# Six branch-gate weights as a seven-product stage ahead of attention, the norm of the mixing in place, fill units and modulation columns dealt out anew

## The chip, the cores and the metric

One Trainium2 chip, one of its cores. The time is device microseconds (us) for one launch, which computes one layer of the model below. Several runs of a kernel give a median; besides them one execution was recorded by the profiler, and all durations and counts of instructions are from that one.

Engine names as in the profile: PE is TensorE (matmuls), PEld its loading of weights, DVE is VectorE, ACT is ScalarE, POOL is GpSimd, SP is SyncE, which issues most of the transfers. An engine takes its instructions in the order in which the program has put them, so an instruction that waits holds back all that stands behind it on its engine.

## The reference

One inference step of one trunk layer, for 640 tokens (128 of a prompt and 512 latents), a model width of 1024, and a feed-forward width of 2816. All inputs are float32.

```python
x = x + 0.5 * m[2] * swiglu(rmsnorm(x, g[0]) * (1 + m[1]) + m[0], ffn1)   # FFN 1
hh = rmsnorm(x, g[1]) * (1 + m[4]) + m[3]          # the norm of the mixing
mq, mk, mv, mo, mg, dq, dk, dv, gm, gd = split_cols(hh @ w_in)
dq, dk = rmsnorm(dq, g_qn), rmsnorm(dk, g_kn)      # then rope_2d for the latents
att = diff_attention(dq, keys, vals, lam)          # 8 heads, 2 softmaxes each, 5 query blocks of 128
hm  = mlstm, forward and backward, on mq, mk, mv with gates mg; 4 heads, chunks of 128
hm  = rmsnorm(hm) * sigmoid(mo)
y   = sigmoid(gm) * (hm @ w_br_m) + sigmoid(gd) * (att @ w_br_d)
x   = x + m[5] * (y @ w_out)
x   = x + 0.5 * m[8] * swiglu(rmsnorm(x, g[2]) * (1 + m[7]) + m[6], ffn2)  # FFN 2
```

m are nine modulation vectors, silu(c) @ w_ada + b_ada, one set for the prompt and one for the latents. Of the products of hh, each of mq, mk, mv, mo, gm, gd is 1024 wide. gm and gd, the branch gates, are only needed in y, at the end of the mixing.

## The kernel before

**Numbers.** Each float32 matrix is split into a high and a low part of the type fp32r, H = copy(x) on ACT and L = x - H on DVE, and a product is three matmuls, H·H, H·L and L·H, into one accumulation (`mm3`, `into`). hh is held as hH and hL, features on the 128 partitions, 8 k-tiles by 640 tokens, in two halves of 320 tokens (`HALF`).

**Weights** come in granules of 1024 x 256 (raw, 1 MB), which are loaded by a DMA, split by one ACT copy and one DVE subtraction, and used as a feature granule or as a token granule. A feature granule has four units of 24 matmuls of 320 columns (`feat_unit`, names ps_p); a token granule has five units of 24 matmuls of 256 columns (`tok_unit`, ps_t). A unit ends with an evacuation of its result from its bank to memory.

**Seven-product form** (class `HalfStep`, `products` L441). In the up stage of FFN 1 and in FFN 2 a granule of 256 features by 640 tokens by 1024 is computed as 2 x 2 blocks in Winograd's form with seven products instead of eight: 84 matmuls of 320 columns (ps_f) instead of 96. For that, sums and differences are needed: four of the operand, once (`operand_sums`, tiles S, 128x640), and four of each weight granule (`Granule.parts`: wB, wC and three differences in place in raw; `Granule.sums`: the last split, ww or wL). They are made on DVE and ACT while the granule before it is being multiplied. Results leave through `done(mt, hf, p, u)`, a copy or a sum with a saved part u.

**Stages**, in the order of TensorE's queue:
1. The opening (0 to 76 us): modulation and the norm of FFN 1.
2. FFN 1 up (76 to 340), then down (340 to 465). While it runs, DVE makes modulation columns too (`Columns`, L720): each of 56 tiles is loaded as 128x1024 and takes a pair of DVE instructions of that size. 14 are placed in the up stage, 18 in the down granules, 14 in attention and 10 in the memory phase (`columns.place(n)`, `columns.tile()`).
3. The norm of the mixing. `to_mixing` (called for each of 8 features tiles d and both halves) gathers squares; x is stored in x_dram with two transfers, one for each half. `norm2` calls `norm_apply` for each d and half: nt = x · scale · rstd on DVE, hH = nt + shift on ACT, hL = nt + shift - hH on DVE. The second half of that runs among the first token units (`norm2_second`).
4. The first query and key projections, as groups of token units (`tok_group`, q0 and k0), their norms and rotations (`qk_norm_rope`, L1290; "rope" below) and tables for them, then the sixteen small products of the mLSTM's gates (`gate_products`, mg, not the branch gates).
5. Attention (518 to 1075): eight heads of five query blocks. For each block TensorE makes scores, the transposes of the block before (`turn`, ps_wT) and its values (`values`, ps_o); between, ACT makes exponentials and DVE the minima (`mn`), the mixing of both softmaxes (`mix`, p) and the turns' copies. Scores stand in banks of their own, which are free again when the exponentials have read them.
6. The memory phase (1075 to 1250): the mLSTM's cells, with fill units between.
7. Branch outputs, w_out (1250 to 1413), FFN 2 (1413 to 1836).

**Fill units** (class `Fill`). The other projections (v, the later q and k, mq, mk, mv, mo, gm, gd) stand in one queue of granules, and `fill.units(n)` puts their next n units on TensorE, so that it has work while DVE and ACT make the softmax. How many stand where is a hand-written table `UNITS`: for each head a pair for every query block (units before and after `mix` and `values`), and a last entry for the end of the head. `fill.ahead()` splits the next granules' weights, which puts a DVE subtraction of 128x2048 (wL) into DVE's queue.

```python
for qi in range(5):
    n = UNITS[hd][qi]
    ... H.scores(qi); H.turn(qi - 1); H.soft(qi)
    aside(hd, qi, 0)            # a modulation tile, in some blocks
    fill.units(n[0])
    ... H.mix(qi); H.values(qi - 1)
    ... heads[hd + 1].pack()    # at qi == 3: queries and keys of the next head
    fill.units(n[1])
    fill.ahead()
```

Where text stands as `with tc.issue_after(i)` or `with written()`, it fixes that the instructions come behind others in their engine's queue; the rest is ordered by a scheduler as the program is built.

Of the kernel before, what the change touches and what calls it, by code (L numbers as in the profile page):

```python
# [31 lines left out]
def tile_trunk(ctx: ExitStack, tc: tile.TileContext, a: dict):  # L32
# [187 lines left out]
    def norm_apply(x, n, m_shift, hf, d, rs, hH, hL, tmp):  # L220
        c0 = hf * HALF
        shift = m_of(m_shift)
        for s0, s1, j in SEGS[hf]:
            t = tmp.tile([128, HALF], F32, tag="nt", name="nt", bufs=2)
            tv = t[:, : s1 - s0]
            stt(tv, x[d][:, s0:s1], scale[:, n, d, j : j + 1], rs[:, s0 - c0 : s1 - c0], ALU.mult, ALU.mult)
            sh = shift[:, d, j : j + 1]
            act(hH[:, d, s0:s1], tv, AF.Identity, bias=sh)
            ins = stt(hL[:, d, s0:s1], tv, sh, hH[:, d, s0:s1].bitcast(F32), ALU.add, ALU.subtract)
        return ins.ins  # L230

# [94 lines left out]
    class HalfStep:  # L326
        def __init__(self, n, fp, tmp, psum, w1, w3, w2, n_plain):

            self.n_plain = n_plain
            self.fp, self.tmp, self.psum, self.w1, self.w3, self.w2 = fp, tmp, psum, w1, w3, w2  # L330
            hm = [hp.tile([128, 2, 2, 4, HALF], F32R, tag=t, name="hm") for t in ("hH", "hL")]

            self.part = {(0, 0): hm[0][:, 0], (1, 0): hm[0][:, 1], (1, 1): hm[1][:, 0], (0, 1): hm[1][:, 1]}
            self.g_dram = dp.tile([4 if n_plain == FB else 7, 128, 2, FB, HALF], F32, name=f"g_dram{n}")
            self.up = [
                Granule(4, lambda raw, src=src: dma(raw, src)) for b in range(1, FB) for src in (w1[b], w3[b])
            ]

        def hh(self, k, hf):
            p = self.part[k // 4, hf]  # L340
            return p[:, 0, k % 4], p[:, 1, k % 4]


        def plain(self, p, w, f, hf, k):

            col = k * 256 + f * 128
            mm3(p, w[0][:, col : col + 128], w[1][:, col : col + 128], *self.hh(k, hf), k == 0, k == KT - 1)

        def begin_gated(self, b):
            self.Q, n = (PLAIN_Q, 4) if b < self.n_plain else (Q, 8)  # L350
            self.SO = self.fp.tile([128, 8, HALF], F32, tag="SO", name="SO")[:, :n]

        def silu_tile(self, f, hf):
            return self.tmp.tile([128, HALF], F32, tag=("nsq", "nt")[f], name="s", bufs=2)

        def gate_plain(self, f, hf, p):
            s = self.silu_tile(f, hf)
            self.at_act = act(s, p[0], AF.Silu)
            tt(vec, self.SO[:, self.Q[f, hf]], p[1], s, ALU.mult)

        def operand_sums(self, pair):

            SS = {i: self.fp.tile([128, 2, 4, HALF], F32R, tag=f"s{i}", name="S") for i in (S1, S2, S3)}
            SS[S4] = self.part[0, 1]
# [42 lines left out]
        def store_g(self, SO, b):  # L407

            n = 4
            if b >= self.n_plain:  # L410
                self.gated_sums(SO)
                n = 7
            for tag, c0, c1 in (("gA", 0, 4), ("gB", 4, 7)):
                if c0 < n:
                    g = self.fp.tile([128, 2, c1 - c0, HALF], F32R, tag=tag, name="g")
                    act(g[:, 0], SO[:, c0:c1], AF.Copy)
                    tt(vec, g[:, 1], SO[:, c0:c1], g[:, 0].bitcast(F32), ALU.subtract)
                    for i in range(2):
                        nc.sync.dma_start(out=self.g_dram[c0:c1, :, i, b, :].rearrange("s p n -> p s n"), in_=g[:, i].bitcast(F32))

        def gated_sums(self, SO):
            tt(vec, SO[:, S1], SO[:, A21], SO[:, A22], ALU.add)
            tt(vec, SO[:, S3], SO[:, A11], SO[:, A21], ALU.subtract)
            tt(vec, SO[:, S2], SO[:, S1], SO[:, A11], ALU.subtract)
            tt(vec, SO[:, S4], SO[:, A12], SO[:, S2], ALU.subtract)


# [13 lines left out]
        def products(self, work, between, then=(), ahead=None, prepared=False):  # L441
# [14 lines left out]
            for i, (gr, A, done, used) in enumerate(work):  # L456
# [14 lines left out]
                X, Y, Z = acc_tile(psum), acc_tile(psum), acc_tile(psum)  # L471
                into(X, A11, True)
# [38 lines left out]
        def add(self, p, u):  # L511
            t = self.tmp.tile([128, HALF], F32, tag="nrt", name="t")
            tt(vec, t, p, u, ALU.add)
            return t

# [221 lines left out]
    with ExitStack() as ph:  # L737
# [254 lines left out]
        def modulation(i, at):  # L992
# [10 lines left out]
            elif i < 28:  # L1003
                if (i, at) == (20, 0):
# [168 lines left out]
    ap = att.enter_context(tc.tile_pool(name="att", bufs=1))  # L1173
# [6 lines left out]
    def gate_products():  # L1180
        raw = load(rawp, [128, KT, 128], a["w_g"], tag="raw", name="wg_raw")
        wgH = ap.tile([128, KT, 128], F32R, tag="kH", name="wgH")
        wgL = ap.tile([128, KT, 128], F32R, tag="kL", name="wgL")
# [106 lines left out]
    def qk_norm_rope(raw, tab):  # L1290
        A, B, g = tab
        sq = ap.tile([128, 5, 256], F32, tag="pk", name="sq", bufs=2)
        act(sq, raw, AF.Square)
        ss = ap.tile([128, 20], F32, tag="ss", name="ss", bufs=2)
        vec.tensor_reduce(out=ss, in_=sq.rearrange("p t (g d) -> p (t g) d", d=64), axis=AX.X, op=ALU.add)
        rs = rstd_of(ap, ss, 1.0 / 64, [128, 20], "qk")
        r3 = raw.rearrange("p t (g d) -> p (t g) d", d=64)
        tt(vec, r3, r3, rs[:, :, None].to_broadcast([128, 20, 64]), ALU.mult)
        sw = ap.tile([128, 4, 256], F32, tag="pk", name="sw", bufs=2)
# [15 lines left out]
    def project_q(pr):  # L1315
        def make():
            q_tok[pr] = t = ap.tile([128, 5, 256], F32, tag="qtok", name="q_tok")

            def evac(p, i):
                act(t[:, i, :], p, AF.Copy)  # L1320
                if i == 4:
                    qk_norm_rope(t, tabs[0])

            return evac

        return a["w_dq"][pr], make

    def project_k(pr):
        def make():
            k_tok[pr] = t = ap.tile([128, 5, 256], F32, tag="ktok", name="k_tok")  # L1330

            def evac(p, i):
                act(t[:, i, :], p, AF.Copy)
                if i == 4:
                    qk_norm_rope(t, tabs[1])
                    nc.sync.dma_start(out=a["new_k"][:, pr * 256 : (pr + 1) * 256], in_=t[:, 4, :])

# [18 lines left out]
    class Head:  # L1356
# [5 lines left out]
        def pack(self):  # L1362
            self.pack_queries(ap, 2)
            self.pack_keys()

        def pack_queries(self, pool, bufs):
# [3 lines left out]
            self.qpk = pool.tile([128, 5, 4, 64], F32R, tag="pk", name="qpk", bufs=bufs)  # L1370
# [70 lines left out]
        def mix(self, qi):  # L1441
# [3 lines left out]
            stt(r, sm[:, 0:1], nlam, rc[:, 1:2], ALU.mult, ALU.mult)  # L1445
# [34 lines left out]
        def finish(self):  # L1480
            aT = ap.tile([128, T], F32, tag="asq", name="aT")
            for i0, n in ((0, 4), (4, 1)):
# [3 lines left out]
                act(aT[:, i0 * 128 : (i0 + n) * 128], p.rearrange("p a b -> p (a b)")[:, : n * 128], AF.Copy, scale=gs)  # L1486
            nc.sync.dma_start(out=aT_dram[:, self.hd, :], in_=aT)


    (src_q, e_q), (src_k, e_k) = project_q(0), project_k(0)  # L1490
    e_q, e_k = e_q(), e_k()
    w_q = split_w(src_q)
    with tc.issue_after(stats[1].at_act.ins), tc.issue_after(stats[1].at_vec.ins):
        w_k = split_w(src_k)

    def norm2_second(k):
        if k == 2:
            box["normed"] = norm2(psum, 1)

    tok_group(psum, [(w_q, 0, e_q), (w_q, 1, e_q)], norm2_second)  # L1500
    tok_group(psum, [(w_k, 0, e_k), (w_k, 1, e_k)], lambda k: None)
    with tc.issue_after(box["normed"]):
        ps_g, gate_step = gate_products()

    tab0 = ap.tile([128, 4, 4, 64], F32, tag="pk", name="tab0", bufs=2)
    cosT, sinT, lamv = tab0[:, 0], tab0[:, 1], tab0[:, 2]
    g_q, g_k = (load(ap, [128, 64], a[n].partition_broadcast(128), name=n) for n in ("g_qn", "g_kn"))
    ts(g_q, g_q, -0.125, ALU.mult)
    with tc.issue_after(box["normed"]):
        nc.sync.dma_start(out=cosT, in_=a["cos"])  # L1510
        nc.sync.dma_start(out=sinT, in_=a["sin"])
        nc.sync.dma_start(out=lamv, in_=a["lam"].partition_broadcast(128))
        gs = load(ap, [128, 1], a["g_sub"], name="gs")
        ts(gs, gs, 1.0 - LAM_INIT, ALU.mult)

        ldot = ap.tile([128, 2], F32, name="ldot")
        for i in range(2):
            vec.tensor_tensor_reduce(
                out=tab0[:, 3, i, :], in0=lamv[:, 2 * i, :], in1=lamv[:, 2 * i + 1, :], op0=ALU.mult, op1=ALU.add,
                scale=1.0, scalar=0.0, accum_out=ldot[:, i : i + 1],  # L1520
            )
        lexp = ap.tile([128, 2], F32, name="lexp")
        act(lexp, ldot, AF.Exp)
# [695 lines left out]
```

## Time and profile before

| | |
|---|---|
| median of three runs | 1840.3 us (1836.87 to 1843.62) |
| the profiled execution's own time | 1838.32 us |
| its span in the profile | 1836.5 us |
| TensorE clock granted, mean | 0.998 |
| busy: PE, DVE, ACT | 98%, 70%, 46% of the span |
| instructions: PE, DVE, ACT | 12,678, 2,110, 1,451 |
| HBM over the span | 162 GB/s |

The page of the profile lists busy time by engine, the span in 40 slices, the chain of work that ended last, and the groups of instructions by program line, with their form: output<-inputs, partitions x elements, type, count. Other views of the same trace are used below: busy time by stretches of the span; groups by line with each form apart; waits by the tile that was waited for and the engine that delivered it (time in us, count, longest); the instructions of a stretch one by one, start and duration first, with a wait in square brackets; and the chain that ended last in its order of time, each piece with its start, its length and how many instructions it holds. A helper records most operations, so L75 is every matmul, L78 every transpose, L51 every ACT operation, L54 every DVE tensor_tensor, L57 every scalar_tensor_tensor: the tile's name tells them apart. TensorE's matmuls overlap in the records, so their mean durations don't add up to its time.

### The profile page before, as it was taken

Reading aid. Unit: us, or ns where it says so; the run is one execution under the profiler, and the core shown is the slowest. Engines: PE = TensorE matmul, PEld = TensorE weight load, DVE = VectorE, ACT = ScalarE, POOL = GpSimd, SP = SyncE. Lnnn points to the kernel's source line nnn. Section 1 sums busy time; section 2 is a strip of 40 time slices with the busy share of each in tenths; the row PEclk is TensorE's granted clock in tenths of the full one; section 3 lists DMA queues with packets and bytes.
Section 4 is the critical chain, followed back from the end, with each engine's and each line's share of the span. In section 5 each row is a group of like instructions: output and inputs, shape, how many; then the busy total and the mean of one; then the engine's idle time right before and its main releaser. Section 6 shows DMA issues by size and latency. Waiting matters only on the chain.

```text
span 1836.5 us, 30726 instructions
## 1 busy us (share of the span) xinstructions
PE 1802.6 (98%) x12678; PEld 1764.6 (96%) x12678; DVE 1282.8 (70%) x2110; ACT 844.2 (46%) x1451; POOL 30.9 (2%) x55
## 2 busy tenths in 40 slices
PE   7999999999999999999999999999999999999999
PEld 5999999999999999999999999999999999999999
DVE  5899886577785767765745457874456878887575
ACT  4644444112554444544544455565235555554232
POOL 0000001010000000000000000000000000000000
PEclk9999999999999999999999999999999999999999
DMA  7364457964324233232222255564532345447872
GB/s 290 120 222 164 172 176 273 379 212 152 110 103 146 96 117 105 104 103 82 71 75 88 76 179 161 189 226 178 182 134 86 133 153 188 170 166 260 313 289 84
DMA packets 127902, 299.83 MB, mean 163 GB/s; under 512 B 9553, under 2 KB 90705, under 8 KB 114961
## 3 DMA queue, kind: packets, MB, share of 16 engines
q1 hardware_dynamic: 118498, 257.49, 40.7%
q0 software_dynamic: 9264, 40.37, 6.0%
q8 instruction: 100, 1.64, 0.4%
q14 instruction: 40, 0.33, 0.1%
HBM read 234.20 MB, written 63.63 MB: 162 GB/s over the span
## 4 chain that ended last, share of the span: by engine, by line
PE 83%; DVE 7%; DMA 6%; ACT 2%; issue 1%; SPq 0%; DVEq 0%; ACTq 0%
PE ps_f L75 40%; PE ps_p L75 22%; PE ps_t L75 12%; PE sc L75 2%; PE ps_o L75 2%; DMA ada<-csil_dram 1%; DVE ww L54 1%; PE ps_n L75 1%; DMA raw_a<-in_w_ada_k 1%; PE ps_wT L78 1%; PE ps_qkT L78 1%; DMA raw<-in_w3a 1%; DVE raw_a L720 1%; DMA P<-nm_dram 1%; PE ps_u L75 1%
## 5 line engine op out<-in xcount | busy, mean ns | idle before, releaser
L75 PE MATMUL ps_f<-S,ww 128*128 128x320 f32 x1956 | 314.3, 310 | 6.8 <-DVE ww L54 3.7
L75 PEld LDWEIGHTS ps_f<-S,ww 128*128 128x128 f32 x1956 | 293.1, 188 | 9.7 <-DVE ww L54 6.9
L75 PE MATMUL ps_p<-hH,wH 128*128 128x320 f32 x864 | 273.3, 316 | 2.0 <-ACT num L51 0.7
L75 PE MATMUL ps_p<-hH,wL 128*128 128x320 f32 x864 | 267.0, 309 | 0.0
L75 PE MATMUL ps_p<-hL,wH 128*128 128x320 f32 x864 | 266.9, 309 | 0.0
L75 PE MATMUL ps_f<-hm,ww 128*128 128x320 f32 x1236 | 194.3, 309 | 2.4 <-DVE ww L54 2.1
L75 PEld LDWEIGHTS ps_f<-hm,ww 128*128 128x128 f32 x1236 | 184.4, 188 | 3.0 <-DVE ww L54 2.4
L75 PE MATMUL ps_t<-wH,hH 128*128 128x256 f32 x640 | 185.3, 290 | 1.0 <-DVE x L57 1.0
L51 ACT ACTIVATE ww<-raw 128x2048 fp32r<-128x2048 f32 (+1 forms) x61 | 114.1, 1870 | 150.0 <-PE ps_f L75 86.3
L75 PE MATMUL ps_t<-wH,hL 128*128 128x256 f32 x640 | 181.2, 283 | 0.0
L75 PE MATMUL ps_t<-wL,hH 128*128 128x256 f32 x640 | 180.9, 283 | 0.0
L75 PEld LDWEIGHTS ps_p<-hH,wH 128*128 128x128 f32 x864 | 162.4, 188 | 3.4 <-ACT num L51 1.1
L75 PEld LDWEIGHTS ps_p<-hL,wH 128*128 128x128 f32 x864 | 162.4, 188 | 0.5
L75 PEld LDWEIGHTS ps_p<-hH,wL 128*128 128x128 f32 x864 | 162.2, 188 | 0.0
L54 DVE TENSOR_TENSOR ww<-raw,ww 128x2048 fp32r<-128x2048 f32 (+1 forms) x61 | 136.3, 2235 | 35.0 <-ACT ww L51 35.0
L75 PE MATMUL ps_f<-hm,wB 128*128 128x320 f32 x984 | 157.6, 309 | 0.0
L75 PEld LDWEIGHTS ps_f<-hm,wB 128*128 128x128 f32 x984 | 147.7, 188 | 0.0
L54 DVE TENSOR_TENSOR wL<-raw,wH 128x2048 fp32r<-128x2048 f32 x49 | 112.2, 2290 | 39.0 <-ACT wH L51 38.3
L75 PEld LDWEIGHTS ps_t<-wH,hH 128*128 128x128 f32 x640 | 122.3, 191 | 2.0 <-issue 1.2
L54 DVE TENSOR_TENSOR raw<-raw 128x1024 f32<-128x1024 f32 x141 | 121.7, 863 | 1.8
L75 PEld LDWEIGHTS ps_t<-wH,hL 128*128 128x128 f32 x640 | 122.4, 191 | 0.5 <-DVE hL L57 0.5
L75 PEld LDWEIGHTS ps_t<-wL,hH 128*128 128x128 f32 x640 | 122.5, 191 | 0.2
(294 smaller groups left out, 3185.8 us busy)
## 6 DMA issues: line engine op xcount, KB each, us to landing
g_dram<-g SPq DMA_DIRECT2D x44, 640.0 KB, 5.9
raw_a<-in_w_ada_c SPq DMA_DIRECT2D x24, 512.0 KB, 4.1
raw<-in_w1b SPq DMA_DIRECT2D x11, 1024.0 KB, 4.9
raw<-in_w3b SPq DMA_DIRECT2D x11, 1024.0 KB, 4.9
raw<-in_w1a SPq DMA_DIRECT2D x10, 1024.0 KB, 4.8
raw<-in_w3a SPq DMA_DIRECT2D x10, 1024.0 KB, 6.4
ada<-in_w_ada_c POOLq DMA_DIRECT2D x18, 512.0 KB, 4.9
hm<-g_dram POOLq DMA_DIRECT2D x7, 1280.0 KB, 10.5
```

Of the source, the lines that this page charges most:

```text
L51: return placed(nc.scalar.activation(*args, **kw))
L54: return placed(eng.tensor_tensor(out=out, in0=in0, in1=in1, op=op))
L75: tc.keep_in_program_order(nc.tensor.matmul(*args, **kw))
L78: tc.keep_in_program_order(nc.tensor.transpose(*args, **kw))
L720: placed(vec.tensor_tensor_reduce(out=junk, in0=raw, in1=self.csil[:, v, :], op0=ALU.mult, op1=ALU.add, scale=1.0, scalar=0.0, accum_out=m ...
```

## The change

1. **Six granules of the branch gates** (gd and gm, column groups 0, 1 and 2 of four) leave the fill queue and the memory phase's units and become a stage of their own, in seven-product form, after `gate_products` and before attention. `HalfStep`'s methods for it go into a base class `Winograd`; a new class `Gates` uses them. In each of its first two granules one matmul more is issued, into a bank that is overwritten (`narrow=2`). Operand sums are made of the normed x, which is held in place for that.
2. **The norm of the mixing** (`norm2`): no `norm_apply`. x is multiplied by rstd in place in pairs of d (4 DVE instructions of 128x640 for each half), ACT makes hH from it with scale and bias, x itself is scaled and shifted in place (first half on ACT, second on DVE), and hL = x - hH in pairs. x_dram is stored in eight parts, one for each pair of d and half, as soon as the pair's residuals are there.
3. **Tables and the ropes of q0 and k0** wait in a list and are issued in the new stage, behind the weight splits of its granules.
4. **Modulation columns**: 21 tiles instead of 18 in the down granules of FFN 1, 11 instead of 14 in attention, 10 in the memory phase as before.
5. **Fill queue** in a new order. v0, mo0, mv0, mq0, q1 and so on come in attention; mk3, mo2, mo3, gm3 and gd3 are left for the memory phase (5 granules, 20 units, as many as before, where mk3 is now evacuated by ACT). Nine units stand ahead of head 0's first block instead of seven, and `UNITS` is written anew with fewer units for each head.
6. **Packing**: both parts of head 0's pack are issued at once; the next head's pack comes at block 4 before `mix` for odd heads instead of at block 3.

```diff
-    class HalfStep:
+    class Winograd:
...
+                if i < narrow:
+                    mm(Y, gr.w[A11][0][0], A(A11)[:, 0, 0], start=True, stop=True)
                 into(X, A11, True)
...
+    class HalfStep(Winograd):
...
-                    columns.place(18, csil, load_columns)
+                    columns.place(21, csil, load_columns)
                 columns.tile(hs.at_vec)
-                if at and i in (22, 25):
+                if at and i < 25:
                     columns.tile(hs.at_vec)
...
-            if stats[hf].n == KT:
-                dma(x_dram[:, :, half(hf)], box["x"][1][:, :, half(hf)])
+            if d % 2:
+                dma(x_dram[:, d - 1 : d + 1, half(hf)], box["x"][1][:, d - 1 : d + 1, half(hf)])
...
         def norm2(psum, hf):
             rs = stats[hf].rstd(psum)
-            for d in range(KT):
-                ins = norm_apply(x, 1, 3, hf, d, rs, *hh2, ntmp)
-            return ins
+            xa, (hH, hL), shift = box["x"][1], hh2, m_of(3)
+            for g in range(4):
+                xs = xa[:, 2 * g : 2 * g + 2, half(hf)]
+                tt(vec, xs, xs, rs[:, None, :].to_broadcast([128, 2, HALF]), ALU.mult)
+                for d in (2 * g, 2 * g + 1):
+                    for s0, s1, j in SEGS[hf]:
+                        xd, sc, sh = xa[:, d, s0:s1], scale[:, 1, d, j : j + 1], shift[:, d, j : j + 1]
+                        act(hH[:, d, s0:s1], xd, AF.Identity, scale=sc, bias=sh)
+                        if hf == 0:
+                            act(xd, xd, AF.Identity, scale=sc, bias=sh)
+                        else:
+                            ts(xd, xd, sc, ALU.mult, sh, ALU.add)
+                ins = tt(vec, hL[:, 2 * g : 2 * g + 2, half(hf)], xs, hH[:, 2 * g : 2 * g + 2, half(hf)].bitcast(F32), ALU.subtract)
...
-        columns.place(14, csil, load_columns, 1)
+        columns.place(11, csil, load_columns, 1)
...
+    class Gates(Winograd):
+        def __init__(self, fp, tmp, psum):
+            self.fp, self.tmp, self.psum = fp, tmp, psum
+            self.part = {(kh, hf): Of(kh, hf) for kh in range(2) for hf in range(2)}
+            self.work = [
+                [Granule(4, lambda raw, src=src[g]: dma(raw, src)), lambda i: self.ops[i], self.done(dst, g), lambda i: None]
+                for g in range(3) for src, dst in ((a["w_gd"], gd_dram), (a["w_gm"], gm_dram))
+            ]
+        def done(self, dst, g):
+            def f(mt, hf, p, u):
+                t = self.tmp.tile([128, HALF], F32, tag=("nsq", "nt")[mt], name="g_out", bufs=2)
+                if u is None:
+                    act(t, p, AF.Copy)
+                else:
+                    tt(vec, t, p, u, ALU.add)
+                nc.sync.dma_start(out=dst[:, 2 * g + mt, half(hf)], in_=t)
+            return f
...
     tok_group(psum, [(w_q, i, e_q) for i in (2, 3, 4)], lambda k: None)
+    G.work[0][0].load()
+    with tc.issue_after(box["normed"]):
+        third, fourth = G.operand_sums(lambda r: box["x"][1][:, 2 * r : 2 * r + 2, :])
+        third()
+        fourth()
     tok_group(psum, [(w_k, i, e_k) for i in (2, 3, 4)], lambda k: None)
     for k in range(KT):
         for hf in range(2):
             gate_step(hf, k)
+    G.work[1][0].load()
...
+    def between(i, at):
+        if at and i < 4:
+            with tc.issue_after(G.work[i + 1][0].split_at):
+                (lambda: None, tables, *ropes)[i]()
...
+    G.products(G.work, between, narrow=2)
-    fill.units(2)
-    heads[0].pack_keys()
-    heads[0].queries()
+    heads[0].pack()
     fill.units(3)
+    heads[0].queries()
+    fill.units(2)
     heads[0].keys(0)
-    fill.units(1)
+    fill.units(2)
     heads[0].keys(1)
...
-    fill.units(1)
+    fill.units(2)
...
-        if part == 0 and (hd in (1, 2, 3) and qi > 0 or hd == 0 and qi > 2):
+        if part == 0 and (hd in (2, 3, 4, 5) and qi in (1, 2) or (hd, qi) in ((1, 1), (2, 3), (4, 3))):
             with written():
                 columns.tile()
...
+    two, one = (1, 1), (1, 0)
     UNITS = {
-        0: ((2, 1), (1, 1), (1, 2), (2, 2), (2, 0), (2, 1, 1)), 1: ((2, 1), (1, 1), (1, 1), (1, 1), (1, 0), (1,)),
-        2: ((2, 1), (1, 1), (1, 1), (1, 1), (1, 1), (1, 1, 1)), 3: ((2, 2), (1, 1), (1, 1), (1, 1), (1, 1), (1,)),
+        0: (two, two, two, (1, 2), one, (1, 1, 1)), 1: ((2, 1), (2, 1), one, one, one, (1,)),
+        2: (two, two, two, two, one, (1, 1, 1)), 3: ((2, 1), (2, 1), two, one, one, (1,)),
+        4: (two, two, two, (1, 2), one, (1, 1, 1)), 5: ((2, 1), (2, 1), two, one, one, (1,)),
+        6: (one,) * 5 + ((0, 0, 0),), 7: (one,) * 4 + ((0, 0),),
     }
-    UNITS.update({4: UNITS[2], 5: UNITS[3], 6: ((2, 1), (1, 1), (1, 1), (1, 1), (1, 0), (1, 1, 1)), 7: ((2, 1), (1, 1), (1, 1), (1, 0), (1, 0))})
...
+            if qi == 4 and odd and hd < 7:
+                with written():
+                    heads[hd + 1].pack()
             with written():
                 H.mix(qi)
...
-            if qi == 3 and hd < 7:
+            if qi == 3 and not odd:
                 with written():
                     heads[hd + 1].pack()
...
-            fill.units(2)
-            fill.drain(1)
+            fill.drain(5)
...
-    for g in range(2, 4):
-        fill.granule(a["w_gm"][g], feat_units(psum, gate_evac(mp, gm_dram, g)))
-        fill.granule(a["w_gd"][g], feat_units(psum, gate_evac(mp, gd_dram, g)))
```

More of the change, by code (lines that the diff above doesn't have):

```diff
@@ L439, in copy_of, with products @@
             return t
-        def products(self, work, between, then=(), ahead=None, prepared=False):
+        def products(self, work, between, then=(), ahead=None, prepared=False, narrow=0):
             n = len(work)
@@ L1496, in norm2_second @@
[L1496 to L1507, printed above, removed]
@@ new lines, in projections @@
+    def projections(pr):
+        token(project_q(pr))
+        token(project_k(pr))
+    token(project_v(0))
+    open_gate(0, lambda: ap)
+    values_of(0)
+    queries_of_memory(0)
+    projections(1)
+    keys_of_memory(0)
+    token(project_v(1))
+    queries_of_memory(1)
+    keys_of_memory(1)
+    projections(2)
+    values_of(1)
+    token(project_v(2))
+    values_of(2)
+    open_gate(1, lambda: ap)
+    projections(3)
+    values_of(3)
+    token(project_v(3))
+    queries_of_memory(2)
```

300 lines of the change are left out of this document (159 added, 141 removed).

## The prediction

> **What bounds the kernel now.** I read the page first, then busy time by stretch.
>
> ```profile
> span 1836.5 us, 30726 instructions
> PE 1802.6 (98%) x12678; PEld 1764.6 (96%) x12678; DVE 1282.8 (70%) x2110; ACT 844.2 (46%) x1451; POOL 30.9 (2%) x55
> PEclk9999999999999999999999999999999999999999
> ...
> core 0: us, PE busy (x) PEld busy (x) DVE busy (x) ACT busy (x) POOL busy (x), PEclk, DMA share, GB/s
> 76.00:340.00 264.00, 258.50 (x1746) 255.82 (x1745) 211.96 (x269) 120.16 (x165) 13.56 (x23) 1.00 0.61 213
> 530.00:567.00 37.00, 35.27 (x255) 34.49 (x254) 30.74 (x50) 21.03 (x37) 0.00 (x0) 1.00 0.32 110
> 567.00:1075.00 508.00, 506.19 (x3935) 499.24 (x3935) 308.49 (x463) 241.26 (x481) 0.00 (x0) 1.00 0.28 95
> 1075.00:1250.00 175.00, 172.30 (x1037) 158.64 (x1035) 126.20 (x366) 108.71 (x258) 0.00 (x0) 1.00 0.61 202
> ```
>
> TensorE is the bound: 34 us idle in 1836.5. In attention (530 to 1075) it is idle 1.73 + 1.81 = 3.5 us while DVE is busy 339 of 545 us (62%). So a matmul removed there is worth its full spacing, as long as the chains that the fill units cover don't come to the surface. The spacing comes from the chain that ended last, whose pieces give time and count; the waits say what TensorE's idle time was.
>
> ```profile
> 350.64 113.49 PE ps_f L75 x772
> 751.91 5.74 PE ps_t L75 x48
> 1299.37 91.76 PE ps_p L75 x624
> ...
> PE ps_f L75 <- DVE ww L54: 5.8, 4, 2.1
> PE ps_wT L78 <- DVE p L57: 3.5, 3, 1.7
> ```
>
> 113.49 / 772 = 91.76 / 624 = 147 ns per 128x320 matmul, in both forms; 5.74 / 48 = 120 ns per 128x256. (The groups' mean of 309 ns counts overlap twice.) So a feature unit of 24 matmuls is 3.5 us, a token unit 2.9.
>
> **1. The products.** Six granules go from 96 to 84 matmuls each, and the first two get one extra: -72 + 2 = -70. The order of the changed kernel's TensorE instructions shows just that (12,174 to 12,104). 70 x 147 ns = **-10.3 us**, all of it on the path, since TensorE is. [...]
>
> **2. Feeding the new stage.** 506 matmuls, 74 us. DVE's work for it, and for the norm and the modulation below:
>
> ```profile
> L54 DVE TENSOR_TENSOR raw<-raw 128x1024 f32<-128x1024 f32 x141 | 121.7, 863 | 1.8
> L54 DVE TENSOR_TENSOR wL<-raw,wH 128x2048 fp32r<-128x2048 f32 x49 | 112.2, 2290 | 39.0 <-ACT wH L51 38.3
> L54 DVE TENSOR_TENSOR wB<-raw,wB 128x1024 fp32r<-128x1024 f32 x49 | 59.7, 1218 | 4.9 <-ACT wB L51 4.9
> L54 DVE TENSOR_TENSOR wC<-raw,wC 128x512 fp32r<-128x512 f32 x49 | 33.5, 683 | 2.7 <-ACT wC L51 2.7
> L54 DVE TENSOR_TENSOR S<-x,S 128x640 fp32r<-128x640 f32 x12 | 9.5, 815 | 0.8 <-ACT S L51 0.8
> L54 DVE TENSOR_TENSOR t<-ps_f,u 128x320 f32<-128x320 f32 x53 | 25.7, 485 | 18.6 <-PE ps_f L75 16.4 <-ACT u L51 2.1
> L1295 DVE TENSOR_REDUCE ss<-sq 128x20 f32<-128x1280 f32 x8 | 11.8, 1477 | 0.0
> L63 DVE TENSOR_SCALAR x<-x,scale,mod 128x192 f32<-128x192 f32 (+1 forms) x32 | 9.8, 357 | 0.0
> L720 DVE CUSTOM_DVE_ANT_0 raw_a<-raw_a,csil 128x1024 bf16<-128x1024 f32 x48 | 58.3, 1215 | 2.8 <-DMA raw_a<-in_w_ada_c 2.6
> ```
>
> A granule's split is 1.22 + 0.68 + 3 differences (0.86 each at most) + 2.29 = 6.8 us, and two evacuations of 0.49 bring it to 7.8, against 84 x 147 ns = 12.3 us of TensorE. Into the same stage fall the two deferred ropes, each 1.48 + 1.49 + 0.43 + 3 x 1.22 + small ones = 7.8 us (rows below), and the tables, some 3. In all about 64 of 74 us, 86%. The up stage of the first FFN (76 to 340) is the nearest stage: DVE at 80% there, and TensorE lost 5.5 us over 21 granules, 0.26 each. Walked in the queue's order, each granule's sums are ready before its second product, by margins of 0.5 us (second granule) to 5. Taken: **+0.6**; bounds 0 and +6.3 (rival B).
>
> Its start: the sixteen operand instructions (13 us of DVE) and the first split come behind the second half's norm. Before, that norm's last low part ends on DVE at 501.3:
>
> ```profile
> 487.93 0.68 DVE L57 SCALAR_TENSOR_TENSOR nt<-x,scale,ry 128x192 f32<-128x192 f32 x2
> ...
> 500.68 0.68 DVE L57 SCALAR_TENSOR_TENSOR hL<-nt,mod,hH 128x192 fp32r<-128x192 f32 x2
> ...
> 517.92 5.75 PE ps_t L75 x48
> ```
>
> In place it costs 4 x 0.8 (the products with rstd, in pairs) + 16 x 0.31 (scale and shift, 9.8 / 32) + 4 x 0.8 (low parts) = 11.4 us instead of 13.4; but the first low part comes only after all four products, so the third token group starts about 1.4 us later and catches up. From 499 DVE needs 1.2 + 13 + about 3.7 to the first granule's sums: 517. The stage starts where the value's first unit did, 517.9, and wants those sums 12 matmuls later: 2 us of margin. x_dram's stores now stand ahead of the in-place product; each leaves after its residual, and the rstd chain behind hides them. Taken: 0; -1 to +3.
>
> **3. Modulation.** Three column pairs (2 x 1.2 us of DVE each) move from attention into the last down granules of the first FFN. DVE was waiting there for loads as long as that, and the wanted splits come at their time. 0; at most +2.
>
> **4. Attention.** 24 feature units leave (84 us of TensorE), and 11 instead of 14 column pairs and 21 splits stay. What must be covered, from a stretch with one unit in a query block:
>
> ```profile
> 1041.13 0.39 PE L75 MATMUL sc<-kH,qT 128*128 128x512 f32 x1
> ...
> 1042.53 0.82 PE L78 MATMUL ps_wT<-ident,p 128*128 128x128 f32 x6
> 1046.70 1.50 PE L75 MATMUL ps_o<-v_tok,wT 128*128 128x128 f32 x12
> ...
> 1053.15 1.76 DVE L1430 TENSOR_REDUCE mn<-sc 128x2 f32<-128x1536 f32 x1 [4.56 <-PE sc L75]
> 1056.85 0.17 DVE L1444 RECIPROCAL rc<-sm 128x2 f32<-128x2 f32 x1 [1.94 <-ACT p L51]
> 1057.31 1.02 DVE L57 SCALAR_TENSOR_TENSOR p<-p,r,p 128x768 f32<-128x768 f32 x1
> 1059.13 2.29 DVE L54 TENSOR_TENSOR wL<-raw,wH 128x2048 fp32r<-128x2048 f32 x1
> 1061.34 0.42 DVE L1430 TENSOR_REDUCE mn<-sc 128x2 f32<-128x256 f32 x1
> ```
>
> From the end of a block's scores, minimum and exponentials free the score banks after 3.7 us (1053.15 to 1056.85) and the mixed weights are there after 5.2. With one feature unit TensorE comes back to the scores after 0.7 (turn) + 3.5 + 1.5 (values) = 5.7 us and to the turn after 7.1: 1.9 us of slack, 1.3 with a token unit. So one unit is enough by itself, and the 2.29 us split, queued ahead of a minimum (the last two rows), is not quite covered.
>
> The tight places are heads 1, 3 and 5, where two projections' ropes fall in:
>
> ```profile
> 780.44 1.49 DVE L54 TENSOR_TENSOR k_tok<-k_tok,ry 128x1280 f32<-128x1280 f32 x1
> 781.98 0.42 DVE L54 TENSOR_TENSOR k_tok<-k_tok,g_kn 128x256 f32<-128x256 f32 x1
> 783.51 1.21 DVE L54 TENSOR_TENSOR sw<-sw,ropeBk 128x1024 f32<-128x1024 f32 x1
> ```
>
> Before, they have two units in nearly each block; now one in blocks 3 and 4. DVE's order there, from the end of block 3's scores: minimum 1.8, rstd 0.4, k_tok 1.5 + 0.4, r and mixing 1.4; then values 0.4, two rope products 2.4, block 4's minimum 0.4, cached keys 0.7, third product 1.2, next queries 0.8, the last mixing 0.7: 12.1 us to the weights of block 4. TensorE: turn 0.7, unit 2.9, values 1.5, scores 0.5, turn 0.7, unit 2.9, values 1.5 = 10.7. It waits 1.4 us in each of the three heads, 4.2. Between heads 6 and 7 no unit stands between the last turn and the next scores (key copies, about +0.8), and none in head 7's block 4 (+0.9). With 0.6 for splits ahead of a minimum: 6.5 us after, against 3.5 before. Before's longest wait is not among the 6.5:
>
> ```profile
> 550.44 2.58 DVE L1234 TENSOR_TENSOR_SCAN lf<-keep,m,u 4x512 f32<-4x512 f32 x2
> ...
> 557.03 0.88 PE L78 MATMUL ps_wT<-ident,p 128*128 128x128 f32 x6 [1.73 <-DVE p L57]
> ```
>
> The gate rows' scans held up head 0's first mixing; now nine units, not seven, stand ahead of head 0 and DVE's order has all the rows ahead of the first minimum. **+3.0**; bounds -3.5 (none left) and rival C.
>
> **5. The memory phase** keeps 20 units; eight of them are now evacuated by DVE and an exponential instead of a copy, 8 x 0.5 us on engines at 72% and 62%. **+0.4**; 0 to +2.
>
> **Sum**: -10.3 + 0.6 + 0 + 0 + 3.0 + 0.4 = -6.3 us. The profiled execution took 1838.32 us (span 1836.5 and 1.8 around it): 1832.0. Its time is 2.0 below the median of the runs, 1840.3; against the median, **1834.0**.
>
> **Rivals.** About 0.3%, 5.5 us, is what a measurement of this kernel can tell from no change.
>
> A, all kept: the waits found above are all absorbed and before's 3.5 us go too: -10.3 - 3.5 = 1826.5, with part of it 1829. For it: chains in such queues shift rather than add up. Against: DVE's share in attention rises from 62% to 69%, (339 - 6 x 2.3 - 3 x 2.4) / (545 - 84), and the 3.5 us had more cover.
>
> B, the stage is DVE's: first sums 4 us later than walked (2 us lost) and then three granules with ropes in their queue each 1.4 us late: with item 2 at +6.3, -0.6: 1839.7. For it: 86%, and the FFN's 5.8 us of waits for ww are of this kind. It decides where the first sums end more than 2 us late.
>
> C, slower: splits decide attention. Of 21 splits each put ahead of a minimum holds TensorE by 2.29 - 1.3 = 1.0 us, 21 us on top of the sum: 1855; with half of them, 1844.5. It passes break-even at 6.3 us more of waits than forecast, and shows as slower from 11.8. For it: the wL row that holds up the minimum at 1061.34. Against: most splits fall in blocks with two or three units, whose slack is over 4 us.
>
> [...]
>
> That the change does not do what it says is excluded by the instruction count.
>
> **Chances.** Forecast 0.45 (its own range 1831 to 1837; two thirds of it below 1834.8), A 0.25, B 0.14, C 0.14, D 0.02. Faster by over 0.3%: 0.25 + 0.30 = 0.55; within: 0.15 + 0.14 + 0.01 = 0.30; slower: 0.15. The range leaves out A's end and C beyond its half: 1827 to 1843.
>
> **What would show it.** Right: TensorE's instructions 70 fewer; a stretch of about 74 us of ps_f ahead of the first scores with under 1.5 us idle; attention some 80 us shorter; TensorE's waits for DVE p 4 to 8 us, at the last turns of heads 1, 3 and 5. Wrong: waits for ww above 3 us in the new stage (B), waits for p or at the score banks above 15 us (C), or under 2 (A).

## The result, and the profile after

The changed kernel takes 1843.95 us (median of 20 runs, 1838.1 to 1847.9), the kernel before 1839.9 (20 runs): a ratio of 1.002, with an interval of 1.0012 to 1.0028. It is slower by some 4 us, where 6.3 us faster was forecast; the time lies just outside the range. The profiled execution took 1844.68 us.

The page of the changed kernel:

```profile
span 1842.9 us, 30690 instructions
PE 1799.4 (98%) x12608; PEld 1759.5 (95%) x12608; DVE 1319.0 (72%) x2148; ACT 868.2 (47%) x1490; POOL 32.4 (2%) x58
```

Seventy TensorE instructions fewer, as forecast, and 6.4 us more. The windows below are cut at the same landmarks of TensorE's queue in both kernels: the new stage, attention, the memory phase. Columns as in the prediction: stretch, its length, then the busy time of PE, PEld, DVE, ACT and POOL. Before:

```profile
517.80:1076.70 558.90, 554.71 (x4299) 546.74 (x4298) 349.13 (x526) 268.40 (x532) 0.00 (x0) 1.00 0.28 95
1076.70:1259.80 183.10, 181.05 (x1097) 167.62 (x1097) 132.86 (x383) 116.20 (x270) 0.00 (x0) 1.00 0.60 199
```

After:

```profile
522.60:596.80 74.20, 74.20 (x508) 74.20 (x508) 55.93 (x78) 37.69 (x57) 0.00 (x0) 1.00 0.47 157
596.80:1085.70 488.90, 476.00 (x3724) 464.16 (x3722) 317.22 (x490) 248.70 (x503) 0.00 (x0) 1.00 0.26 88
1085.70:1266.90 181.20, 179.89 (x1097) 168.18 (x1097) 136.99 (x391) 116.01 (x269) 0.00 (x0) 1.00 0.61 199
```

The column to read is PEld. While TensorE streams, one weight load follows on the other (74.20 of 74.20 us in the stage), so what PEld's idle time grows by is the best measure of what TensorE lost. PE's own column hides a part, because the modelled end of the last matmul reaches into each wait: in attention after, PE is idle 488.90 - 476.00 = 12.9 us, PEld 24.7. Before, PEld is idle 558.90 - 546.74 = 12.2 us in attention, a part of which stands in stretches without any wait. After, it is idle 0 in the stage and 488.90 - 464.16 = 24.7 in attention. Stage and attention together are 563.1 us against 558.9: +4.2. The 70 products give -10.3, the idle loads +12.5, and a stretch of half clock in attention (last section) 1.7; that is +3.9 of the 4.2.

The rest of the span: the two parts of the first FFN +4.5 us, of which 3.4 are two stretches of half clock and 0.7 a wait; the memory phase -1.9; everything else within 0.7. In all, past the opening and up to the last matmul, the profiled execution after had three stretches of half clock (from 92.7, 352.1 and 1041.6, 3.41 us each) and the one before had none: 3 x 1.7 = 5.1 of the 6.4 us between them. So this pair of executions exaggerates the clock's part. Over more runs it nearly vanishes: the mean granted clock is 0.9953 in the 20 runs after and 0.9957 in 29 runs of before, 0.8 us. Without the clock this pair is 1.3 us apart and the medians are about 3, so some 2 us of the medians' difference has no place in these two profiles. The loss that counts is attention's 12.5.

TensorE's waits in attention, after (before, the first of these rows was 3.5 us in 3 waits, and there was no other):

```profile
PE ps_wT L78 <- DVE p L57: 8.1, 11, 1.0
PE sc L75 <- ACT p L51: 1.7, 2, 1.0
PE ps_p L75 <- DVE stage L61: 0.7, 1, 0.7
PE ps_qkT L78 <- DVE kp L54: 0.7, 1, 0.7
PE ps_o L75 <- ACT wT L51: 0.5, 1, 0.5
PE sc L75 <- DVE kH L1416: 0.2, 1, 0.2
```

They are 11.9 us by these rows and 15.0 by the matmuls' starts (the spacing over that of the same form elsewhere, places above 0.3 us; 4.0 before). Taken one by one from the starts, in order of time: the last turns of heads 0 to 5, 0.95 to 1.13 each, 6.3 together; the start of a block's scores in heads 1 and 6, 2.0; block 2's turn in heads 3 and 5, 2 x 1.05; from head 6's last turn to head 7's first scores 2.0; head 7's block 4, 1.7; the wait for `stage` ahead of head 0, 0.9. Two of the last turns, on VectorE. Head 3:

```profile
853.64 0.42 DVE L1440 TENSOR_REDUCE mn<-sc 128x2 f32<-128x256 f32 x1
853.98 0.68 DVE L54 TENSOR_TENSOR kL<-ck,kH 128x512 fp32r<-128x512 f32 x1
854.58 1.22 DVE L54 TENSOR_TENSOR k_tok<-k_tok,sw 128x1024 f32<-128x1024 f32 x1
855.71 0.82 DVE L54 TENSOR_TENSOR qpk<-q_tok,qpk 128x640 fp32r<-128x640 f32 x1
...
856.90 0.35 DVE L57 SCALAR_TENSOR_TENSOR p<-p,r,p 128x128 f32<-128x128 f32 x1
```

And head 4:

```profile
920.14 2.29 DVE L54 TENSOR_TENSOR wL<-raw,wH 128x2048 fp32r<-128x2048 f32 x1 [1.25 <-ACT wH L51]
922.35 0.42 DVE L1440 TENSOR_REDUCE mn<-sc 128x2 f32<-128x256 f32 x1
922.68 0.68 DVE L54 TENSOR_TENSOR kL<-ck,kH 128x512 fp32r<-128x512 f32 x1
...
924.10 0.35 DVE L57 SCALAR_TENSOR_TENSOR p<-p,r,p 128x128 f32<-128x128 f32 x1
```

TensorE in head 3, from the end of block 4's scores: block 3's turn, one unit, block 3's values, and the wait at the last turn.

```profile
851.00 0.28 PE L75 MATMUL sc<-kL,qT 128*128 128x256 f32 x1
851.25 0.87 PE L78 MATMUL ps_wT<-ident,p 128*128 128x128 f32 x6
...
854.84 1.50 PE L75 MATMUL ps_o<-v_tok,wT 128*128 128x128 f32 x12
857.31 0.33 PE L78 MATMUL ps_wT<-ident,p 128*128 128x128 f32 x1 [0.96 <-DVE p L57]
```

Head 3 is the chain that the prediction walked: rope, cached keys and packing stand between block 4's minimum and its mixing. Head 4 has no rope; there it is the split of the next granule's weights, queued ahead of the minimum and itself 1.25 us late for ScalarE's half of the split. That is read from the order of VectorE's queue; no run took a split out. With one unit between block 4's scores and the last turn, TensorE is there 4.8 us after the scores, and p is about 1 us later in both.

### The profile page after: what moved, and what is told of

It is laid out like the page before. It is cut to its first block, busy times and chain, and to the rows that moved or that the text cites. A ratio compares the mean times of both kernels' runs of the same rounds, so it can differ in the third digit from the quotient of the medians.

```text
span 1842.9 us, 30690 instructions
## 1 busy us (share of the span) xinstructions
PE 1799.4 (98%) x12608; PEld 1759.5 (95%) x12608; DVE 1319.0 (72%) x2148; ACT 868.2 (47%) x1490; POOL 32.4 (2%) x58
## 4 chain that ended last, share of the span: by engine, by line
PE 77%; DVE 8%; DMA 7%; issue 3%; ACT 3%; SPq 1%; POOL 0%; POOLq 0%; DVEq 0%; ACTq 0%
PE ps_f L75 38%; PE ps_p L75 18%; PE ps_t L75 10%; PE ps_n L75 2%; PE sc L75 2%; DMA ada<-in_w_ada_c 2%; DMA g_dram<-g 2%; DVE ww L54 1%; PE ps_u L75 1%; PE ps_o L75 1%; DMA raw_a<-in_w_ada_k 1%; PE ps_wT L78 1%; PE ps_qkT L78 1%; DMA raw<-in_w3a 1%; DVE wL L54 1%
## 5 line engine op out<-in xcount | busy, mean ns | idle before, releaser
L75 PE MATMUL ps_f<-S,ww 128*128 128x320 f32 x2172 | 350.7, 311 | 5.6 <-DVE ww L54 3.7
L75 PEld LDWEIGHTS ps_f<-S,ww 128*128 128x128 f32 x2172 | 327.4, 189 | 8.3 <-DVE ww L54 6.8
L75 PE MATMUL ps_p<-hH,wH 128*128 128x320 f32 x672 | 213.2, 317 | 2.3 <-ACT aT L51 0.9
L75 PE MATMUL ps_p<-hH,wL 128*128 128x320 f32 x672 | 208.2, 310 | 0.0
L75 PE MATMUL ps_p<-hL,wH 128*128 128x320 f32 x672 | 208.2, 310 | 0.0
L54 DVE TENSOR_TENSOR raw<-raw 128x1024 f32<-128x1024 f32 x159 | 137.2, 863 | 2.0
L54 DVE TENSOR_TENSOR wL<-raw,wH 128x2048 fp32r<-128x2048 f32 x43 | 98.5, 2290 | 54.3 <-ACT wH L51 49.1
L75 PEld LDWEIGHTS ps_p<-hH,wH 128*128 128x128 f32 x672 | 126.9, 189 | 3.4 <-ACT aT L51 1.2
L75 PEld LDWEIGHTS ps_p<-hL,wH 128*128 128x128 f32 x672 | 126.8, 189 | 0.5
L75 PEld LDWEIGHTS ps_p<-hH,wL 128*128 128x128 f32 x672 | 126.6, 188 | 0.0
```

Of the source, the lines that this page charges most:

```text
L54: return placed(eng.tensor_tensor(out=out, in0=in0, in1=in1, op=op))
L75: tc.keep_in_program_order(nc.tensor.matmul(*args, **kw))
```

## The experiments

The theory after the result was C: the stage pays in full, and attention gives it back because single blocks have too little between their scores and their turn. The rivals are in the expectations. Each kernel ran in five rounds with the kernel before on the same chip; the ratios are to that.

**One unit moved to block 4.** The changed kernel with other numbers in the table:

```diff
-        0: (two, two, two, (1, 2), one, (1, 1, 1)), 1: ((2, 1), (2, 1), one, one, one, (1,)),
-        2: (two, two, two, two, one, (1, 1, 1)), 3: ((2, 1), (2, 1), two, one, one, (1,)),
+        0: (two, two, two, (1, 1), two, (1, 1, 1)), 1: ((2, 1), (1, 1), one, one, two, (1,)),
+        2: (two, two, two, one, two, (1, 1, 1)), 3: ((2, 1), (2, 1), one, one, two, (1,)),
```

Head 4 is as head 0, head 5 as head 3.

> The changed kernel with the same units dealt otherwise: in heads 0, 2 and 4 one unit of block 3 and in heads 1, 3 and 5 one unit of block 1 or 2 goes to block 4, between the values and the last turn. Theory C (cover): the changed kernel gives its 10.3 us back because single blocks of attention have lost the unit that covered their softmax; the waits at the last turn, 0.9 us in each of six heads, go, and the blocks that give a unit have slack: 4 to 5 us less than the changed kernel, about 1839.5. Theory L (load): VectorE has too much to do in these heads (splits, modulation columns, ropes), and the wait turns up in the blocks that lost a unit: within 1 us of the changed kernel, 1843 to 1845.

1843.09 us, 1.0019 (1.001 to 1.0028): no gain that can be told. But the halves differ. In heads 0, 2 and 4 the last turn's wait is gone and nothing came for it. In heads 3 and 5 it is gone too, and two larger ones stand where the unit was taken, 2.1 us at block 3's scores and 1.65 at the turn behind them: the ropes of the next pair fall into block 2, and one unit doesn't cover them. In head 1 it stays. The time is L's, the places are as C says for the even heads: C holds by block, and L is right that heads 1, 3 and 5 had no unit to give away in these blocks.

**Four granules in the stage.**

```diff
-                for g in range(3) for src, dst in ((a["w_gd"], gd_dram), (a["w_gm"], gm_dram))
+                for g in range(2) for src, dst in ((a["w_gd"], gd_dram), (a["w_gm"], gm_dram))
```

gd and gm of group 2 stand in the fill queue again, and the table has one unit more in block 4 of heads 0 to 5 and of head 7 and one between heads 6 and 7.

> Only four granules in the seven-product stage (46 products saved, 6.8 us); gd and gm of group 2 go back to the fill queue as eight units, one in block 4 of heads 0 to 5 and of head 7 and one between heads 6 and 7. Tables and ropes come one granule earlier. Theory C: the spacing lost in attention, 15.6 us after and 4.0 before, falls to about 6; about 1837, 3 us below the kernel before and 7 below the changed one. Theory P (the loss is not in the cover, but in the parts moved elsewhere: norm in place, columns, deferred ropes): the changed kernel plus the 3.5 us of 24 products given back, 1847.

1841.98 us, 1.0009 (1.0 to 1.0019). P's 1847 is out: giving 24 products back did not make the kernel slower (the median is 2 us lower, which the intervals hardly tell from no change). But C's 1837 is missed as well:

```profile
520.70:570.30 49.60, 49.60 (x341) 49.60 (x340) 39.89 (x59) 25.27 (x39) 0.00 (x0) 1.00 0.48 161
570.30:1082.60 512.30, 503.02 (x3915) 493.51 (x3914) 323.92 (x495) 254.97 (x515) 0.00 (x0) 0.99 0.27 91
```

PEld is idle 18.8 us in attention, not 24.7: eight units took 5.9 us of waits away, where I had expected 9, and the granted clock in it is 0.99 (1.00 after). The last turns wait no more; the waits at the middle blocks of heads 3 and 5, at head 6's scores and between heads 6 and 7 are left.

**Eight units from the memory phase.**

```diff
     values_of(1)
+    open_gate(2, lambda: ap)
...
-    open_gate(2, lambda: mp)
...
-            fill.drain(5)
+            fill.drain(3)
...
-    fill.pace(1.4, 1)
+    fill.pace(0.84, 1)
```

The table is that of the run with four granules.

> All six granules stay in the stage; the eight units for attention (same places as with four granules) are taken from the memory phase instead, which keeps 12 units of 20 at a slower pace. Theory C, with a memory phase that has cover to spare: attention's waits fall by 9 us and nothing else moves: 1835. Rival M (the memory phase needs its units, VectorE being busy 76% of it): its 28 us shorter stretch is then bound by VectorE and gives as much back: 1843 to 1848.

1846.22 us, 1.0037 (1.0024 to 1.0049). Rival M:

```profile
594.40:1105.60 511.20, 502.89 (x3916) 493.75 (x3915) 324.19 (x496) 253.09 (x510) 0.00 (x0) 0.99 0.26 90
1105.60:1267.00 161.40, 154.10 (x907) 139.39 (x906) 125.33 (x384) 109.61 (x260) 0.00 (x0) 1.00 0.61 203
```

Attention's idle loads fall by 7.2 us, to 17.5, and the memory phase's rise by 9.0, from 13.0 to 22.0. With the eight units gone and the pace set to match, it had none to spare.

**Modulation pairs of attention cut short.** The width is 8 for the 11 tiles made in attention alone; all others are made in full.

```diff
-
+        width = None
...
-                        out=junk, in0=raw, in1=self.csil[:, v, :], op0=ALU.mult, op1=ALU.add, scale=1.0, scalar=0.0,
+                        out=junk[:, : self.width], in0=raw[:, : self.width], in1=self.csil[:, v, :][:, : self.width], op0=ALU.mult, op1=ALU.add, scale=1.0, scalar=0.0,
...
         columns.place(11, csil, load_columns, 1)
+        columns.width = 8
...
     columns.place(10, csil2, load_columns_raw, 1)
+    columns.width = None
```

> The 11 modulation tiles made in attention are cut to 8 of their 1024 columns, loads and order kept: 27 us of VectorE's work leave attention out, and eleven of the modulation columns are not computed in full. Theory C: the columns lie in blocks with two units, so the waits stay: at most 2 us less, 1842 to 1844. Theory L: VectorE's load decides, and at least half of the 11.6 us of new waits go: 1836 to 1839.

1841.26 us, 1.0002 (0.9994 to 1.0011), 2.7 us below the changed kernel by the medians:

```profile
594.80:1080.00 485.20, 474.03 (x3723) 462.87 (x3722) 295.54 (x490) 248.69 (x503) 0.00 (x0) 1.00 0.26 89
```

VectorE is 22 us less busy, and the idle loads go from 24.7 to 22.3. What went are the two waits at block 2's turn in heads 3 and 5, where a pair stood ahead of that block's mixing; all the last turns wait as before. The time lies between the two forecasts (C 1842 to 1844, L 1836 to 1839). By the waits, a lighter VectorE alone does not cure the last turns; of the column pairs, only the two in the wrong place cost something, 2.1 us by the matmuls' starts.

**Packing back in block 3.**

```diff
-            if qi == 4 and odd and hd < 7:
-                with written():
-                    heads[hd + 1].pack()
...
-            if qi == 3 and not odd:
+            if qi == 3 and hd < 7:
```

> The changed kernel with the next head's pack back at block 3 for odd heads too, as in the kernel before. Theory K (packing ahead of the last mixing makes the last turns of heads 1, 3 and 5 late): VectorE's 0.8 us leaves that chain, 2 to 2.5 us less, 1841.5. Theory C: the copies only move to block 3's chain, which has one unit as well: within 1 us of the changed kernel, 1843 to 1845.

1853.0 us, 1.0068 (1.0054 to 1.0082): 9 us slower than the changed kernel, which neither theory had. (Between the profiled executions it is 9.0 us too; by the mean granted clocks of the two spans, 0.993 and 0.995, some 4 of it are the clock's, an estimate, and attention's is 0.99 where it is 1.00 after.) ScalarE in head 3's blocks 3 and 4:

```profile
857.32 0.38 ACT L51 ACTIVATE stage<-ps_t 128x256 f32<-128x256 f32 x1 [3.06 <-PE ps_t L75]
858.91 1.36 ACT L51 ACTIVATE kpk<-k_tok 128x640 fp32r<-128x640 f32 x2 [1.21 <-DVE k_tok L54]
860.18 0.85 ACT L51 ACTIVATE wT<-ps_wT 128x512 f32<-128x512 f32 x2
```

The packing's copy waits for the rope's last product, and the copy of block 3's turns stands behind it; TensorE's values wait 3.5 us for wT in heads 3 and 5 and 2.3 in head 1. So the packing's move to block 4 was needed in this order of units, and the chain that it lengthens by 0.8 us is the smaller price.

**The stage in plain form.** The six granules stand first in the fill queue, as plain feature units:

```diff
-    G.products(G.work, between, narrow=2)
+    for u in range(24):
+        fill.one()
+        if u in (5, 9, 13):
+            (tables, *ropes)[(u - 5) // 4]()
...
```

Not shown are the granules' places in the queue and their evacuation by ScalarE; the operand sums are left out.

> The changed kernel, its six granules at the same place ahead of attention as plain units (96 matmuls each, 576 instead of 506), without operand sums; tables and ropes between them. All theories: the stage takes 576 x 147 ns = 84.5 us instead of 74.2; 10.3 us more than the changed kernel, 1854, if VectorE's sums of the seven-product form were wholly hidden; less than 8 us more if they cost something that the spacing of the stage's matmuls doesn't show. Attention is unchanged.

1854.96 us, 1.0079 (1.0067 to 1.0091): 11.0 us above the changed kernel where 10.3 were expected. The stage with attention:

```profile
520.20:1091.00 570.80, 558.79 (x4299) 547.17 (x4297) 337.23 (x506) 270.41 (x534) 0.00 (x0) 1.00 0.28 93
```

23.6 us idle, 1.1 less than after, and place by place the same waits. So the form brings its full price, and taking the 24 units out of attention costs what it costs in either form.

**The norm in place alone**, in the kernel before (`norm2` and the stores of x_dram as in the change):

> The kernel before with one part of the change alone: the norm of the mixing in place, with x stored in eight parts. Theories C and the prediction: TensorE's time from the norm's sums to the gate products moves by under 1 us, and the time with it: 1839 to 1841. Theory P (part of the loss is here): 2 us or more above the kernel before, 1842.

1839.61 us, 0.9999 (0.9991 to 1.0008). Nothing lost there.

**The same units, dealt by block.** All six granules in the stage, the same number of units for each head:

```diff
+        0: (two, two, two, (1, 1), two, (1, 1, 1)), 1: ((2, 1), (2, 1), two, one, two, (1,)),
+        2: (two, two, two, one, two, (1, 1, 1)), 3: ((2, 1), (2, 1), two, two, two, (1,)),
...
-                for i in range(5):
+                for i in range(3):
                     fill.one()
```

Head 4 is as head 0, head 5 as head 3, and heads 6 and 7 are as in the change.

> The changed kernel, all six granules in the stage and the same number of units in each head, dealt otherwise: in heads 1, 3 and 5 two of the six units that stand at the head's end go into its blocks, one of them into block 4; in heads 0, 2 and 4 one unit of block 3 goes into block 4. Theory C (cover by block, not by head): the six waits at the last turns (6 x 1.0 us) and the two before block 3's transposes (2 x 1.05) go, about 8 us less than the changed kernel, 1835 to 1837, below the kernel before. Theory N (a head needs its whole number of units, and each unit taken away opens a wait where it stood): the ends of the odd heads wait instead, 1841 to 1844.

1837.61 us, 0.9985 (0.9977 to 0.9994): faster than the kernel before, by C's expectation but for 0.6 us, and N's 1841 is out. The six waits at the last turns are gone:

```profile
PE ps_wT L78 <- DVE p L57: 5.2, 6, 2.4
PE sc L75 <- ACT p L51: 1.0, 1, 1.0
```

The ends of heads 1, 3 and 5 had six units where the even heads' have three, and don't miss two of them. The pairs' waits in heads 3 and 5 (1.05 each) didn't go, and head 1 got one of 2.4 at the turn of block 3, which still has one unit.

**Three waits further.**

```diff
-        0: (two, two, two, (1, 1), two, (1, 1, 1)), 1: ((2, 1), (2, 1), two, one, two, (1,)),
+        0: (two, two, two, (1, 1), two, (1, 1, 1)), 1: ((2, 1), (2, 1), two, two, two, (1,)),
...
-        6: (one,) * 5 + ((0, 0, 0),), 7: (one,) * 4 + ((0, 0),),
+        6: (one,) * 5 + ((0, 1, 0),), 7: (one,) * 4 + ((0, 0),),
...
-                for i in range(3):
+                for i in range(3 if hd == 3 else 2):
                     fill.one()
```

The modulation tiles stand in (head, block) (0, 3), (0, 4), (1, 1), (3, 1), (5, 1) and blocks 1 to 3 of heads 2 and 4.

> The dealt version, three waits further: in head 1 a third unit goes from the head's end into block 3; of heads 3 and 5 the modulation pair of block 2, which stood ahead of that block's mixing, goes to head 0's blocks 3 and 4; one unit of head 5's end goes between heads 6 and 7. Theory C: the waits of 2.5, 1.05, 1.05 and some 1.2 us at these places go, 5 to 6 us less than the dealt version, 1832. Theory N: the shorter ends of heads 1 and 5 wait instead, 1836 to 1838.

1834.97 us, 0.9972 (0.9961 to 0.9983), the fastest of all:

```profile
598.20:1077.10 478.90, 472.49 (x3724) 462.60 (x3723) 319.14 (x490) 244.97 (x500) 0.00 (x0) 1.00 0.26 90
```

16.3 us idle, 8.4 less than after. Its largest waits are now for keys:

```profile
PE sc L75 <- ACT kL L51: 2.9, 3, 2.1
PE sc L75 <- ACT p L51: 1.3, 2, 1.0
PE ps_wT L78 <- DVE p L57: 0.8, 2, 0.5
```

The 2.1 us at the end of head 1, whose six units are now three, is N's wait, once; so by the medians it is 2.6 us less than the dealt version (2.4 by the ratios, whose intervals overlap) and not the 5 to 6 of C.

## Why the prediction was wrong, step by step

1. Products: right. The chain after has the stage as one piece, 74.21 / 506 = 146.7 ns a matmul, and the plain form costs 11.0 us more.

```profile
522.74 74.21 PE ps_f L75 x506
```

2. Feeding the stage: +0.6 forecast, 0.0 measured; no wait in it, with VectorE at 55.93 / 74.20 = 75%, not 86%. The deferred ropes and the rest were hidden. From the norm's sums to the stage's start it is 53.4 us, 53.8 before; in place, the norm costs nothing.

3. Modulation in the down granules: 0 forecast, one wait of 0.74 us for a granule's wB, ahead of which VectorE has a column pair that waited 0.99 us for its load. Right within its bounds.

4. Attention is the step that failed: +3.0 forecast, 12.5 measured. The mechanism was right (p late at the last turn), its places were not. TensorE's waits for p came to 8.1 us, near the "4 to 8" of the forecast, but that is partly luck: three of the six last turns that waited were not among those named. I walked VectorE's order for heads 1, 3 and 5 and said 1.4 us each; it is 0.95 to 1.13 there, and 1.03 each in heads 0, 2 and 4, which I had passed as having no rope. For them I had the slack of a whole block, 1.9 us, with the turn 7.1 us behind the scores; block 4 has 4.8, as its own scores are short and no others follow, and the split of 2.29 us stands ahead of its minimum. All splits together were put at 0.6 us; these three places alone cost 3.1. Not seen were the two pairs of columns ahead of a mixing (2.1) and the score banks in heads 1 and 6 (2.0). Between heads 6 and 7 and in head 7 I had 1.7 and it is 3.7. And the sum was made of wait rows, which are too small here: they rise by 8.4 us (3.5 to 11.9), the matmuls' starts show 11.0 more, the idle loads 12.5. That the same units and all of VectorE's splits, in other places, lose 8.4 us less (16.3 idle in the last run) shows that the places made most of it.

5. Memory phase: +0.4 forecast, -1.9 measured. The kernels with the new queue and all 20 units have 179.9 to 182.8 us there, the two with the old queue 183.1. Which of its edits does that was not tried.

Of the prediction's rivals, C (splits; another C than the cover theory of the experiments) came closest in time (half of it was 1844.5), with a third of its mechanism: splits ahead of three minima, not ten, go with 1 us each. A's reason, that waits in such queues shift rather than add up, did not hold here: 15.0 us of them stood side by side, and 8.3 us by the same working are left in the last dealt version. B's late sums did not happen. D's 0.02 stood for time lost to TensorE's clock: past the opening and up to the last matmul the profile before has no stretch of half clock, the one after has three, 5.1 us. The range ended at 1843, short of C's half, and the time lies 0.95 us above it.

## What to carry to other kernels

When work that covers a chain is taken out, count the cover for each block by itself, from the last instruction that feeds the chain to the first that needs its result, with everything queued on the chain's engines in between: the total of a head or of a stage doesn't show which block waits. A block without its usual rope can still be the tight one, if a split stands ahead of its minimum. And when a large saving gives nothing back, look at where the remaining cover stands before giving up the saving: the same units, and two modulation tiles, in other places were worth 9 us here.

## What the runs showed of the hardware

In the profiles before and after, TensorE's granted clock is 0.50 for one stretch of 6.83 us in the opening (from 15.5 us before, from 17.6 after) and, after, for the three of 3.41 us past it; from the opening's stretch to the last matmul it is 1.00 in all the rest. The stretches of full clock between them are whole multiples of 3.413 us (after 68.27, 256.00 and 686.08, 20, 75 and 201 of them; before 1812.48, 531 of them, up to the half clock behind the last matmul), so in each profile they begin and end on a grid of that period; its place against the span's start differs by 1.2 us between the two. The same wait of 2.1 us in the first FFN, before and after (columns: stretch, length, PE busy and its count, granted clock, DMA share, GB/s):

```profile
340.00:360.00 20.00, 17.88 (x123) 1.00 0.98 355
```

```profile
340.00:360.00 20.00, 17.91 (x112) 0.91 0.98 355
1040.00:1060.00 20.00, 19.67 (x124) 0.91 0.05 17
```

After, the wait (349.4 to 351.5) lay wholly in one period of the grid (348.7 to 352.1), of which PE was busy 39%, and the next ran at half clock, 11 matmuls fewer in the 20 us. Before, it (348.5 to 350.6) lay across two, busy 58% and 80%, and the clock stayed at 1.00. So after, with the half clock behind it, the same wait cost 1.7 us more than its length (3.41 us at 0.50). The row at 1040 is the one in attention: no wait there is over 0.7 us, but those between heads 6 and 7, a place full of transposes, add up, and PE was busy 71% of the period ahead of the stretch. Ahead of the one from 92.7 it was 21%. Periods of 49% before (554.8 to 558.2, with the wait of 1.73 us) and of 61%, 69% and 70% after (from 1471.7, 468.2 and 1069.0) have a clock of 1.00 behind them, so by these two profiles the busy share alone does not tell which period is followed by half clock.
